# Experts ranked by their tokens, with a two-product path for the three smallest, in a two-layer transformer kernel

## The chip, the cores and the metric

The kernel runs on one core of one Trainium2 chip. The metric is the device time of one execution in microseconds (us). Three runs of the kernel before gave 1542.59, 1545.02 and 5386.56 us; their median is 1545.02 us. One further execution was profiled: it took 1542.61 us, and its span from the first to the last instruction is 1540.7 us.

## The reference

The program is a network of two layers on 256 tokens of 1024 channels, all in float32. Each layer is a mixer (two kinds of attention, a convolution, gates, an output product) followed by a feed-forward part. In layer 0 that part is one dense SwiGLU of width 2816; in layer 1 it is a mixture of eight experts of the same width, of which each token takes the two with the highest router logits. The change is in layer 1's feed-forward part:

```
h = rms_norm(x, ffn_norm_g)                       # 256 tokens x 1024
logits = h @ w_router + b_router                  # 256 x 8
top_logits, top_idx = top_k(logits, 2); gates = softmax(top_logits)
for each expert e, on the tokens that chose it:
    y = (silu(xe @ w_gate[e]) * (xe @ w_up[e])) @ w_down[e]
    x[token] += gate[token, e] * y
```

There are 512 choices for eight experts. With the reference's own inputs the experts 0 to 7 are chosen by 55, 77, 81, 111, 36, 59, 35 and 58 tokens.

The weights of one expert are 3 x 1024 x 2816 float32 numbers, 34.6 MB; the eight have 276.8 MB, and each is read once from the chip's memory.

## The kernel before, in words

**Splitting.** Matrix products are made in a float32 mode of TensorE that keeps only part of the mantissa, so each operand is split into a high and a low part, and a product is the sum of three matmuls: high by high, low by high, high by low (`mm3`, lines 379 to 381). The tokens stand still in the array (a 128x128 tile) and 512 columns of weights stream past. The weights' split is made on the core, in pieces: ScalarE (ACT) copies a piece of the raw tile to its high part (line 248) and VectorE (DVE) subtracts to get the low part (line 252). In the profile these are `hi<-raw` and `lo<-raw`.

**The stream of weights.** `_Stream` holds one list of chunks in the order in which they are used. A chunk is 2048 columns on 128 partitions (1 MB), loaded by one DMA from SP's queue into a ring of raw tiles: 5, and 7 more once the dense part is over, in the expert stage 12. A chunk is split in two pieces of `UNIT` = 1024 columns. There are four buffers for high parts and four for low ones (`PART_BUFS`), and `AHEAD` = 3 pieces are split ahead of the one in use. `next` hands out a piece and at once issues the split of the piece three further on. A raw tile comes free when its second low part is made, and only then can SP issue the DMA that refills it.

**The experts.** `route` and its helpers (`turned`, `logits`, `choose`, `place`) make the router's choice at the end of layer 1's mixer and give each token a place among the tokens of its expert (`slots`, `sels`). `moe` then goes through the experts 0 to 7 in order. Each is computed with 128 places, however many tokens it has; a conditional second pass at the end handles an expert with more than 128. For two experts at a time `gather` (line 991) builds one-hot matrices `pm` by comparing places with a row of numbers, and multiplies the split tokens `xhi`, `xlo` by them on TensorE (`xgp`, line 1009). Its result is scaled by the norm's gain and split again (lines 444 and 445, `xg`). `backward` transposes `pm` for the way back.

For each expert, gate and up products come in five blocks of 512 columns and one of 256 of each. A block's gate product `eg` takes 8 steps of 128 channels, 24 matmuls, then 24 for the up product `eu`. ACT makes the silu (line 1074), DVE multiplies gate by up (line 1079), four transposes `eaT` on TensorE (line 1065) turn the result, and ACT and DVE split it (`ehl`). The product with `w_down` then takes 22 steps of two halves, 132 matmuls `ed`. An expert has 396 matmuls of 512 columns and 66 pieces of weights to split. Its result is split (`yhi`, `ylo`) and scattered to the tokens' rows by 8 matmuls `sc`; ACT scales and GpSimd (POOL) adds to `x` (lines 1045, 1046), but for the last expert, where DVE does both.

**Order.** `tick` is called after each piece; `later(n, f)` puts `f` behind the n-th tick from then. So small work, such as transposes, is laid between the matmuls. Instructions of an engine run in the order in which the scheduler put them; TensorE, ACT, DVE, POOL and SP each have their own.

Of the kernel before, what the change touches and what calls it, by code (L numbers as in the profile page):

```python
# [36 lines left out]
MORE_BUFS = 7  # L37
AHEAD = 3
WARM = 7
MOE_SLABS = 8  # L40
SHARE = ((0,0),(1,0),(0,1),(1,1))
OUT_LAST = 3
CONV_RATE = 8 / 3
EARLY = (1, 1)
FIRST_LO = (-1, -1)
# [18 lines left out]
C_DIST = C_IOTA + S  # L64
# [16 lines left out]
def _constants():  # L81
# [14 lines left out]
    c[:, C_IOTA:C_IOTA + S] = k  # L96
    return c
# [17 lines left out]
def _chunks():  # L115
# [13 lines left out]
    def swiglu(key, names, i, by_half):  # L129
# [5 lines left out]
        if by_half:  # L135
            for h in range(2):
                k0s = list(range(0, FT, 4)) if h == 0 else [*range(0, FT - 6, 4), *range(FT - 6, FT, 2)]
                for k0, k1 in zip(k0s, k0s[1:] + [FT]):
                    out.append((key + "_dh", [(wd, i, k0, k1 - k0, h * 512, 512)], k1 - k0, 512))
        else:  # L140
            rows(key + "_d", wd, i, FT)

    for l in range(L):
# [16 lines left out]
        if l == 0:  # L160
            swiglu("f", ("w_ffn_gate", "w_ffn_up", "w_ffn_down"), 0, False)
    first_expert = len(out)
    for e in range(NE):
        swiglu("e", ("w_exp_gate", "w_exp_up", "w_exp_down"), (0, e), e == NE - 1)
    return out, first_expert


def _stream(h):
# [3 lines left out]
    chunks, _ = _chunks()  # L172
    flat = np.empty(sum(P * kn * n for _, _, kn, n in chunks), np.float32)
    at = 0
    for _, parts, kn, n in chunks:
        view = flat[at:at + P * kn * n].reshape(P, kn, n)
        at += P * kn * n
        c = 0
        for name, i, k0, k, c0, w in parts:
            a = h[name][i][k0 * P:(k0 + k) * P, c0:c0 + w]  # L180
            view[:, :, c:c + w] = a.reshape(k, P, w).transpose(1, 0, 2)
            c += w
# [16 lines left out]
class _Stream:  # L199
# [3 lines left out]
    UNIT = UNIT  # L203

    def __init__(self, tc, raw_pool, part_pool, ahead):
# [8 lines left out]
        self.more_pool = None  # L214
        self.hold = None
        self.lo_late = None
        self.turn = -1
        self.made = 0
        self.used = 0
# [8 lines left out]
    def add(self, key, src, kn, n):  # L228

        ci = len(self.plan)  # L230
        self.plan.append((src, kn, n))
        ku = self.UNIT // n
# [3 lines left out]
    def _make(self):  # L236
        nc = self.nc
        key, ci, u, ku, n = self.units[self.made]
        self.made += 1
        src, kn, _ = self.plan[ci]  # L240
        if ci not in self.raws:
            raw = self.raw_tile([P, kn * n])
            nc.sync.dma_start(raw, src)
            self.raws = {ci: raw}
        part = self.raws[ci][:, u * self.UNIT:(u + 1) * self.UNIT]
        hi = self.part_pool.tile([P, self.UNIT], F32R, tag="hi", name="hi")
        lo = self.part_pool.tile([P, self.UNIT], F32R, tag="lo", name="lo")
# [7 lines left out]
        return (key, hi.rearrange("p (k n) -> p k n", n=n), lo.rearrange("p (k n) -> p k n", n=n))  # L255
# [18 lines left out]
    def _fill(self):  # L274
        while (self.made < len(self.units) and self.made - self.used < self.ahead
               and self.units[self.made][0] != self.hold):
            self.queue.append(self._make())

    def next(self, key):
        if not self.queue:  # L280
            self.queue.append(self._make())
        k, hi, lo = self.queue.pop(0)
        assert k == key, (k, key)
        self.used += 1
# [5 lines left out]
def tile_kernel(ctx, tc, x, weights, columns, consts, out, dbg=None):  # L290
# [54 lines left out]
    onesr = cst.tile([P, P], F32R, name="onesr")  # L345
    half = cst.tile([P, 16], F32, name="half")
# [19 lines left out]
    chunks, first_expert = _chunks()  # L366
    places = [0]
    for _, _, kn, n in chunks:
        places.append(places[-1] + P * kn * n)

    def plan_chunks(start):
        for (key, _, kn, n), at in zip(chunks[start:], places[start:]):
            ws.add(key, weights[at:at + P * kn * n].rearrange("(p x) -> p x", p=P), kn, n)

    plan_chunks(0)
# [507 lines left out]
    def route(t, h):  # L883

        if (t, h) == (0, 0):
            rt.update(wrg=moe_weights(), hi=hp.tile([P, TT, D], F32R, tag="hhi", name="xhi"),
                      lo=hp.tile([P, TT, D], F32R, tag="hlo", name="xlo"), xT=[], rs=[], rs2=[], lg=[], late=[], sels=[], picks=[],
                      slots=[])
        if (t, h) == (1, 0):
            turned(0)  # L890
        if (t, h) == (1, 1):
# [4 lines left out]
            rt["late"][1](dve_)  # L896
            place(0)
            choose(1)
            place(1)

    def turned(t):
# [3 lines left out]
        late = rt["late"]  # L905
        if t == 1:
            late.extend(ws.begin(EARLY[0]))
        for q in range(2):
# [4 lines left out]
            (act_.copy if q else dve_.tensor_copy)(tl[:, 4 * q:4 * q + 4, :].rearrange("p k s -> p (k s)"), b)  # L913
        dve_.tensor_scalar(rs, rs, 1.0 / D, EPS, op0=ALU.mult, op1=ALU.add)
        pool_.tensor_tensor(rs, rs, half[:, :1], op=ALU.pow)
        if t == 1:
            late.extend(ws.begin(EARLY[1]))
            late[0](pool_)
# [3 lines left out]
        hi, lo = rt["hi"][:, t, :], rt["lo"][:, t, :]  # L922
        act_.activation(hi, xs[t], AF.Copy)
        pool_.tensor_tensor(lo, xs[t], hi.bitcast(F32), op=ALU.subtract)
        if t == 1:
            late.extend(ws.begin(PART_BUFS - len(late)))
# [42 lines left out]
    def moe():  # L969
        hhi, hlo, rs2, sels, picks, slots = (rt[k] for k in ("hi", "lo", "rs2", "sels", "picks", "slots"))  # L970


# [21 lines left out]
        def gather(e0, s0, late=()):  # L994

            pm = work.tile([P, TT, 2, P], F32R, tag="pm", name="pm", bufs=1)
            for t in range(TT):
                for i in range(2):
                    dve.tensor_scalar(pm[:, t, i, :], con[:, C_IOTA + s0:C_IOTA + s0 + P],
# [199 lines left out]
```

## Time and profile before

| what | value |
|---|---|
| median of three runs | 1545.02 us |
| profiled execution, device time | 1542.61 us |
| its span | 1540.7 us |
| TensorE, matmuls (PE) busy | 1495.4 us, 97% |
| DVE busy | 1236.7 us, 80% |
| ACT busy | 1024.2 us, 66% |
| bytes moved by DMA | 399.73 MB |
| first matmul of the first expert | 749.84 us |
| last `yhi` of the last expert | 1531.47 us |

A duration of a matmul in the profile includes the time in which it overlaps with the next, so the spacing of the starts, not the busy time, tells how fast TensorE goes. "Idle before" is the time that an engine stood still ahead of an instruction, and the name behind the arrow is what ended it.

### The profile page before, as it was taken

To read this page: it belongs to the slowest core of one execution; us is meant where nothing else is said; L and a number is where in the kernel's file an instruction comes from. 1 tells how busy PE (TensorE), PEld (TensorE's weight loads), DVE (VectorE), ACT (ScalarE), POOL (GpSimd) and SP (SyncE) were. 2 spreads that over 40 slices of the span, in tenths; PEclk is the share of its full clock that TensorE was granted. 3 is DMA by queue.
4 is the path that set the end of the run, shared out by engine and by line. 5 is a ranking of instruction groups with operands and counts; after the bars stand their busy time and mean duration, and the time that the engine had idled before them with its cause. 6 is when DMAs were issued, how large, how long until landed. Compare 5 with 4: busy or idle time off the path is not lost.

```text
span 1540.7 us, 19299 instructions
## 1 busy us (share of the span) xinstructions
PE 1495.4 (97%) x7080; PEld 1223.5 (79%) x7080; DVE 1236.7 (80%) x1519; ACT 1024.2 (66%) x1275; POOL 93.0 (6%) x70
## 2 busy tenths in 40 slices
PE   9989999999999989999899999999999999999997
PEld 7867788788887777788788888888878878778786
DVE  5898657655546798666898989989899989899897
ACT  6646653544335557653787888877777777777775
POOL 0200000000000200000100202001010010100100
PEclk9999999999999999999899999999999999999999
DMA  8343345455455343448599989998989989899881
GB/s 353 137 164 137 137 159 190 171 191 184 175 195 183 137 164 111 159 168 316 205 381 369 347 320 363 380 372 338 342 325 369 371 338 352 332 348 379 342 328 44
DMA packets 56551, 399.73 MB, mean 259 GB/s; under 512 B 6400, under 2 KB 6656, under 8 KB 8704
## 3 DMA queue, kind: packets, MB, share of 16 engines
q1 hardware_dynamic: 56160, 398.32, 68.7%
q8 instruction: 57, 0.93, 0.2%
q14 instruction: 46, 0.38, 0.1%
q10 hardware_dynamic: 288, 0.10, 0.0%
HBM read 397.34 MB, written 1.05 MB: 259 GB/s over the span
## 4 chain that ended last, share of the span: by engine, by line
PE 84%; DVE 8%; ACT 4%; POOL 2%; issue 1%; DMA 0%; SPq 0%; DVEq 0%; ACTq 0%
PE ed L379 5%; PE ed L380 5%; PE ed L381 5%; PE eg L381 5%; PE eg L379 5%; PE eg L380 5%; PE eu L381 5%; PE eu L379 4%; PE eu L380 4%; DVE lo L252 3%; PE gt L379 2%; PE gt L381 2%; PE gt L380 2%; DVE acc L539 2%; ACT hi L248 2%
## 5 line engine op out<-in xcount | busy, mean ns | idle before, releaser
L252 DVE TENSOR_TENSOR lo<-raw,hi 128x1024 fp32r<-128x1024 f32 x750 | 906.9, 1245 | 226.3 <-ACT hi L248 207.5
L248 ACT ACTIVATE hi<-raw 128x1024 fp32r<-128x1024 f32 x754 | 770.0, 1057 | 309.2 <-PE ed L380 36.0
L379 PE MATMUL eg<-hi,xg 128*128 128x512 f32 x384 | 153.8, 401 | 0.0
L381 PE MATMUL eg<-lo,xg 128*128 128x512 f32 x384 | 150.4, 392 | 0.0
L380 PE MATMUL eg<-hi,xg 128*128 128x512 f32 x384 | 149.7, 390 | 0.0
L379 PE MATMUL ed<-hi,ehl 128*128 128x512 f32 x352 | 138.2, 393 | 0.0
L380 PE MATMUL ed<-hi,ehl 128*128 128x512 f32 x352 | 137.8, 392 | 0.0
L381 PE MATMUL ed<-lo,ehl 128*128 128x512 f32 x352 | 133.6, 391 | 0.0
L381 PE MATMUL eu<-lo,xg 128*128 128x512 f32 x320 | 126.8, 396 | 6.5 <-DVE lo L252 6.5
L379 PE MATMUL eu<-hi,xg 128*128 128x512 f32 x320 | 125.4, 392 | 0.0
L380 PE MATMUL eu<-hi,xg 128*128 128x512 f32 x320 | 125.0, 391 | 0.0
L539 DVE SCALAR_TENSOR_TENSOR acc<-uT,cols,acc 128x255 f32<-128x255 f32 (+29 forms) x240 | 97.2, 465 | 0.0
L1046 POOL TENSOR_TENSOR x<-x,add 128x512 f32<-128x512 f32 x28 | 54.0, 1958 | 650.1 <-ACT add L1045 650.1
L381 PEld LDWEIGHTS eg<-lo,xg 128*128 128x128 f32 x384 | 72.1, 188 | 15.9 <-DVE lo L252 0.2
L380 PEld LDWEIGHTS eg<-hi,xg 128*128 128x128 f32 x384 | 72.4, 189 | 14.0 <-DVE xg L445 0.2
L379 PEld LDWEIGHTS eg<-hi,xg 128*128 128x128 f32 x384 | 72.2, 188 | 13.4
L381 PEld LDWEIGHTS eu<-lo,xg 128*128 128x128 f32 x320 | 60.1, 188 | 26.1 <-DVE lo L252 12.8
L381 PEld LDWEIGHTS ed<-lo,ehl 128*128 128x128 f32 x352 | 66.1, 188 | 13.7
L379 PE MATMUL gt<-hi,hhi 128*128 128x512 f32 x192 | 76.8, 400 | 0.0
L380 PEld LDWEIGHTS ed<-hi,ehl 128*128 128x128 f32 x352 | 66.2, 188 | 13.2
L379 PEld LDWEIGHTS ed<-hi,ehl 128*128 128x128 f32 x352 | 66.2, 188 | 13.0
L381 PE MATMUL gt<-lo,hhi 128*128 128x512 f32 x192 | 75.6, 394 | 0.0
(273 smaller groups left out, 2489.2 us busy)
## 6 DMA issues: line engine op xcount, KB each, us to landing
raw<-in_weights_dram SPq DMA_DIRECT2D x373, 1024.0 KB, 5.5
raw<-in_weights_dram SPq DMA_DIRECT2D x8, 512.0 KB, 5.3
x<-in_x_dram SPq DMA_DIRECT2D x2, 512.0 KB, 4.3
out_dram<-x SPq DMA_DIRECT2D x4, 256.0 KB, 2.5
att<-in_consts_dram SPq DMA_DIRECT2D x1, 448.0 KB, 6.9
con<-in_consts_dram SPq DMA_DIRECT2D x1, 256.0 KB, 6.2
cols<-in_columns_dram SPq DMA_DIRECT2D x1, 160.0 KB, 7.1
con<-in_consts_dram ACTq DMA_DIRECT2D x1, 64.0 KB, 4.0
```

Of the source, the lines that this page charges most:

```text
L248: ins = nc.scalar.activation(hi, part, AF.Copy)
L252: nc.vector.tensor_tensor(lo, part, hi.bitcast(F32), op=ALU.subtract)
L379: pe.matmul(dst, ahi, whi, start=first, stop=False)
L380: pe.matmul(dst, alo, whi, start=False, stop=False)
L381: pe.matmul(dst, ahi, wlo, start=False, stop=last)
L539: dve.scalar_tensor_tensor(acc[:, c, lag:], uT[:, c, :S - lag], w, acc[:, c, lag:], op0=ALU.mult, op1=ALU.add)
L1046: pool.tensor_tensor(xs[t][:, sl], xs[t][:, sl], add, op=ALU.add)
```

## The change

- **Ranks.** After the routing, `count` ranks the experts on the core: the experts 0 and 1 always get ranks 0 and 1, and the other six follow by falling number of tokens. DVE makes the order (`ranked`) and moves places and gates into it. The experts are computed in the order of ranks 0, 1, 5, 2, 6, 3, 4, 7.
- **Addresses from a register.** From the third expert on, which expert is loaded is known only on the core. SP reads its number from `ranked` into a register (`expert_of`), and the DMAs of that expert take their address from it. The weights of the experts are laid out in an array of their own, one row per expert.
- **64 places, two products.** The experts of ranks 5, 6 and 7 have 64 places. The high and the low part of their tokens stand side by side in the 128 columns of the still operand, so two matmuls, by the high and by the low part of the weights, give all four products. The lower half of the result is then copied by ACT (`low`) and added to the upper half by one matmul with a shifted identity (`fold`). In the down product no fold is needed: the scatter matrix has each place twice. If one of these three has more than 64 tokens, or another expert more than 128, a second pass goes over all eight experts.
- **Pieces of 2048 columns.** The experts' weights are split in pieces of 2048 columns, one per chunk, but for the first four and for the ends of the down product. Six buffers of that size hold three pairs of high and low parts; two pieces are split ahead. The raw ring has 11 tiles instead of 12.
- **The gather takes scaled tokens.** The gain is multiplied into the tokens before they are split (`xgain`, by DVE in `route`, with a table `gain` that one DMA loads). The gather's high and low matmuls go to separate columns of a bank, and one ACT copy of 512 or 384 columns takes both: DVE no longer splits `xg`. But for the first, a gather is spread over four ticks. The subtractions `xlo` move from POOL to DVE, as does the one low part of weights that POOL made there.

Cut to its core (`...` stands for lines left out):

```diff
-MORE_BUFS = 7
-AHEAD = 3
+MORE_BUFS = 6
+MORE_PARTS = 2
+AHEAD = 3 * 1024
+AHEAD_E = 2 * 2048
...
+UNIT_E = 2048
+SHORT = P // 2
+
+RANKS = (0, 1, 5, 2, 6, 3, 4, 7)
+SHORTS = (5, 6, 7)
...
+    def part_tile(self, name):
+
+        n = PART_BUFS + (MORE_PARTS if self.more_parts else 0)
+        self.part_turn = (self.part_turn + 1) % n
+        pool = self.part_pool if self.part_turn < PART_BUFS else self.more_parts
+        return pool.tile([P, UNIT_E], F32R, tag="part", name=name)
...
-            nc.sync.dma_start(raw, src)
+            nc.sync.dma_start(raw, src() if callable(src) else src)
...
+    def expert_of(rank):
+
+        if rank not in order["reg"]:
+            order["reg"][rank] = nc.values_load(order["idx"][0:1, rank:rank + 1], engines=(mybir.EngineType.SP,),
+                                                min_val=0, max_val=NE - 1)
+        return order["reg"][rank]
...
+                    flat = experts[bass.ds(expert_of(rank), 1), at:end].rearrange("o (p x) -> (o p) x", p=P)
...
+        if h == 0:
+            rt["xg"].append(T([P, D], "xgain"))
+        sl = slice(h * 512, (h + 1) * 512)
+        dve_.tensor_tensor(rt["xg"][t][:, sl], xs[t][:, sl], rt["gain"][:, sl], op=ALU.mult)
...
+    def low(t):
+        dve_.tensor_tensor(rt["lo"][:, t, :], rt["xg"][t], rt["hi"][:, t, :].bitcast(F32), op=ALU.subtract)
...
-            late[0](pool_)
...
-        pool_.tensor_tensor(lo, xs[t], hi.bitcast(F32), op=ALU.subtract)
...
-                    split_evac(hi, lo, b[:, j * S:(j + 1) * S], col(R_FG + KT + k))
...
+                    act.activation(xg[kp][:, j, :], b[:, :2 * width], AF.Copy)
...
+            def products(b, whi, wlo, lhs, first, last):
+                if short:
+                    pe.matmul(b, lhs(0), whi, start=first, stop=False)
+                    pe.matmul(b, lhs(0), wlo, start=False, stop=last)
+                else:
+                    mm3(b, lhs(0), lhs(1), whi, wlo, first, last)
...
+                        if k == KT and short:
+                            low = work.tile([P, 512], F32R, tag="low", name="low", bufs=2)
+                            act.activation(low[SHORT:], b[SHORT:], AF.Copy)
+
+                            def folded():
+                                pe.matmul(b, fold[SHORT:], low[SHORT:], start=False, stop=True, skip_group_check=True)
+                                then()
+                            later(2, folded)
...
+            dve.scalar_tensor_tensor(key, b[:, :NE], 8.0, con[:, C_KEY:C_KEY + NE], op0=ALU.mult, op1=ALU.add)
+            dve.max(top, key)
+            dve.max_index(idx, top, key)
...
-        with tc.If(most > P):
-            plan_chunks(first_expert)
-            all_experts(P, gather(0, P))
...
+        with tc.If(most > 0):
+            order["reg"] = {}
+            plan_experts()
+            all_experts(gather([(0, False), (1, False)], order["rest"], True), [0, 1], lambda: order["rest"], ())
```

How the instructions move, at three places. The first is ACT within the gate and up products of one block. Before, in expert 1 (`hi` is a piece of 1024 columns, `ea` the silu, `ehl` the turned block):

```order
L441 ACTIVATE ehl<-eaT 128x512
L248 ACTIVATE hi<-raw 128x1024 x2
L1074 ACTIVATE ea<-eg,rss 128x512
L248 ACTIVATE hi<-raw 128x1024 x6
L441 ACTIVATE ehl<-eaT 128x512
```

And now, in the first expert with 64 places, the third that is computed (`low` is the lower half of a product on its way to the fold):

```order
L1180 ACTIVATE low<-eg 64x512
L509 ACTIVATE ehl<-eaT 128x4x64
L284 ACTIVATE hi<-raw 128x2048
L1210 ACTIVATE ea<-eg,rss 64x512
L284 ACTIVATE hi<-raw 128x2048
L1180 ACTIVATE low<-eu 64x512
L284 ACTIVATE hi<-raw 128x2048 x3
```

Between two blocks stood eight pieces of 1024 columns, and now four or five of 2048; two instructions `low` stand among them.

The second place is DVE at the routing, behind the last residual sum. Before (`fi` and `sel` belong to the choice of the two experts, `slot` to the places, `pm` to the gather):

```order
L195 TENSOR_TENSOR x_89<-x_89,wo 128x512
L195 COPY xTf<-xTr 128x512
L195 CAST fi<-idx 128x2
L195 SCALAR_TENSOR_TENSOR sel_6015<-con,fi,s_6014 128x8
L195 TENSOR_TENSOR lo<-raw,hi 128x1024
L999 TENSOR_SCALAR pm<-con,slot_6036 128x128 x2
L195 TENSOR_TENSOR lo<-raw,hi 128x1024 x2
L445 SCALAR_TENSOR_TENSOR xg_6053<-xgp,cols,xg_6051 128x256 x2
```

And now:

```order
L219 TENSOR_TENSOR xlo<-xgain,xhi 128x1024
L219 TENSOR_TENSOR x_89<-x_89,wo 128x512
L219 TENSOR_TENSOR xgain<-x_89,gain 128x512
L219 COPY xTf<-xTr 128x512
L219 CAST fi<-idx 128x2
L1079 TENSOR_SCALAR pm<-con,slot_5817 128x128 x2
L219 TENSOR_TENSOR xlo<-xgain,xhi 128x1024
L219 TENSOR_TENSOR hilo<-raw,hilo 128x1024 x4
```

Two subtractions `xlo` and the products `xgain` came to DVE; the low part of weights between `sel` and the places went behind `pm`, and the splits of `xg` are gone.

The third place is SP's queue at the start of the third expert, where before the DMAs simply followed one another (`raw<-in_weights_dram` without anything between). Now:

```order
L276 DMA raw<-in_experts_dram 128x1024 x2
L412 TENSOR_LOAD ranked
L412 ISA x2
L276 ISA
L276 DMA raw<-in_experts_dram 128x2048
```

The expert's number is read once per expert, and one further instruction, `ISA`, stands ahead of each DMA.

## Rows read from the trace of the kernel before

**Rows 1.** The page's DMA issues: tiles, queue, count, KB each, us to landing.

```profile
raw<-in_weights_dram SPq DMA_DIRECT2D x373, 1024.0 KB, 5.5
```

**Rows 2.** Stages: from:to us, length, busy us by engine, granted clock, DMA share, GB/s.

```profile
8.00:12.00 4.00, 2.76 (x12) 1.79 (x11) 3.41 (x5) 4.00 (x8) 0.94 (x1) 1.00 1.04 400
...
720.00:730.00 10.00, 10.00 (x50) 8.39 (x49) 4.58 (x6) 2.61 (x4) 0.00 (x0) 1.00 1.01 423
740.00:750.00 10.00, 6.86 (x36) 6.75 (x37) 7.72 (x22) 2.75 (x8) 0.67 (x1) 0.59 0.46 162
800.00:900.00 100.00, 99.63 (x450) 81.94 (x449) 92.94 (x85) 81.45 (x90) 8.48 (x4) 1.00 0.96 359
```

**Rows 3.** Timeline of ACT: the first `yhi` of experts 0 to 4 and 6, start us first.

```profile
842.47 0.60 ACT L441 ACTIVATE yhi<-ed 128x512 fp32r<-128x512 f32 x1 [0.26 <-PE ed L381]
...
942.15 0.60 ACT L441 ACTIVATE yhi<-ed 128x512 fp32r<-128x512 f32 x1 [0.26 <-PE ed L381]
...
1037.13 0.60 ACT L441 ACTIVATE yhi<-ed 128x512 fp32r<-128x512 f32 x1 [0.26 <-PE ed L381]
...
1138.44 1.09 ACT L441 ACTIVATE yhi<-ed 128x512 fp32r<-128x512 f32 x2 [1.39 <-PE ed L381]
...
1235.26 1.09 ACT L441 ACTIVATE yhi<-ed 128x512 fp32r<-128x512 f32 x2 [1.88 <-PE ed L381]
...
1433.54 1.09 ACT L441 ACTIVATE yhi<-ed 128x512 fp32r<-128x512 f32 x2 [1.88 <-PE ed L381]
```

**Rows 4.** Timeline of PE in expert 1's up and gate products.

```profile
900.10 0.39 PE L381 MATMUL eu<-lo,xg 128*128 128x512 f32 x1
...
902.82 0.39 PE L381 MATMUL eg<-lo,xg 128*128 128x512 f32 x1
...
905.09 0.60 PE L1065 MATMUL eaT<-con,ea 128*128 128x128 f32 x4
...
905.45 0.47 PE L379 MATMUL eg<-hi,xg 128*128 128x512 f32 x1
```

**Rows 5.** Groups of DVE, 900 to 1400 us: count, busy us, mean ns, idle before.

```profile
L252 DVE TENSOR_TENSOR lo<-raw,hi 128x1024 fp32r<-128x1024 f32 x333 | 403.7, 1259 | 33.6 <-ACT hi L248 31.4
L1079 DVE SCALAR_TENSOR_TENSOR ea<-eu,rss,ea 128x512 f32<-128x512 f32 x26 | 19.3, 744 | 0.3 <-PE eu L381 0.3
L442 DVE TENSOR_TENSOR ehl<-eaT,ehl 128x512 fp32r<-128x512 f32 x25 | 17.2, 689 | 2.8 <-ACT ehl L441 1.2
...
L442 DVE TENSOR_TENSOR ehl<-eaT,ehl 128x256 fp32r<-128x256 f32 x5 | 2.1, 418 | 0.0
```

**Rows 6.** Timeline of DVE: four low parts back to back.

```profile
1184.03 4.63 DVE L252 TENSOR_TENSOR lo<-raw,hi 128x1024 fp32r<-128x1024 f32 x4 [0.50 <-ACT hi L248]
```

**Rows 7.** Groups of ACT, 900 to 1400 us, columns as in rows 5.

```profile
L248 ACT ACTIVATE hi<-raw 128x1024 fp32r<-128x1024 f32 x334 | 335.8, 1055 | 44.8 <-PE ed L380 24.4 <-PE eg L380 9.7 <-PE eu L380 7.2
L1074 ACT ACTIVATE ea<-eg,rss 128x512 f32<-128x512 f32 x25 | 17.1, 684 | 4.5 <-PE eg L381 4.5
L441 ACT ACTIVATE ehl<-eaT 128x512 fp32r<-128x512 f32 x25 | 14.9, 595 | 41.1 <-PE eaT L1065 39.7 <-PE ed L381 1.4
```

**Rows 8.** Timeline of all engines at the routing, and the first expert matmul.

```profile
735.61 2.36 POOL L195 TENSOR_TENSOR lo<-raw,hi 128x1024 fp32r<-128x1024 f32 x1
735.66 2.33 DVE L195 CAST fi<-idx 128x2 f32<-128x2 uint32 x1
...
738.30 2.39 DVE L195 SCALAR_TENSOR_TENSOR sel<-con,fi,s 128x8 fp32r<-128x8 f32 x1
738.33 2.34 POOL L195 TENSOR_TENSOR xlo<-x,xhi 128x1024 fp32r<-128x1024 f32 x1
...
742.95 0.17 DVE L195 CAST fi<-idx 128x2 f32<-128x2 uint32 x1
...
749.84 0.40 PE L379 MATMUL eg<-hi,xg 128*128 128x512 f32 x1
```

**Rows 9.** Waits of SP's queue, 760 to 1500 us: total us, times, longest.

```profile
SPq L243 <- DVE lo L252: 630.2, 245, 7.7
```

More of the change, by code (lines that the diff above doesn't have):

```diff
@@ L134, in swiglu @@
         proj(key + "_gu", [(wg, i, DFF - 256), (wu, i, DFF - 256)], 256)
[L135 to L141, printed above, removed]
+        rows(key + "_d", wd, i, FT)
     for l in range(L):
@@ L274, in _fill @@
     def _fill(self):
[L275 to L276 removed]
+        while (self.made < len(self.units) and self.units[self.made][0] != self.hold
+               and self.waiting + self.units[self.made][3] * self.units[self.made][4] <= self.ahead):
             self.queue.append(self._make())
@@ L289, in tile_kernel @@
 @with_exitstack
-def tile_kernel(ctx, tc, x, weights, columns, consts, out, dbg=None):
+def tile_kernel(ctx, tc, x, weights, experts, columns, consts, gains, out, dbg=None):
     nc = tc.nc
@@ new lines, in gather, with part @@
+            pts, rss = [], []
+            for fn in late:
+                fn(dve_)
+            for kp in range(KT // 2):
+                if at_once:
+                    piece(kp)
+                else:
+                    later(1 + kp, lambda kp=kp: piece(kp))
+            later(1 if at_once else 1 + KT // 2, lambda: backward(pm, pts, rss))
+            def part(i, q, k):
+                row = xg[k // 2][:, k % 2, :]
+                if pair[i][1]:
+                    return row[:, P:2 * P]
+                at = q * width + i * P if not short else q * (2 * width - P)
+                return row[:, at:at + P]
@@ L1035, in backward, with scatter @@
                 rss.append(r1)
-        def scatter(e, pt, yhi, ylo, h):
+        def scatter(gate, last, pt, yhi, ylo, h):
             sl = slice(h * 512, (h + 1) * 512)
@@ L1111, in moe, with all_experts, of @@
         gs = []
-        def all_experts(s0, got):
-            for e in range(NE):
-                xg, pts, rss = got
-                more = e % 2 and e + 1 < NE
-                nxt = expert(e, xg, pts, rss, lambda: gather(e + 1, s0) if more else None)
-                got = nxt or got
-        first = gather(0, 0, rt["late"][2:])
-        later(2, lambda: gs.extend(weigh()))
-        top = small.tile([P, 1], F32, tag="cnt", name="cnt", bufs=1)
-        cnt = small.tile([P, 1], I32, tag="cnti", name="cnti", bufs=1)
+        def all_experts(got, pair, slots, shorts):
+            ranks = RANKS
+            for p in range(NE):
+                r = ranks[p]
+                part, pts, rss = got
+                gate = (lambda t, r=r: order["gs"][t][:, r:r + 1]) if p >= 2 else (lambda t, r=r: gs[t][:, r:r + 1])
+                nxt = expert(pair.index(r), r in shorts, part, pts, rss, gate, p == NE - 1,
+                             (lambda q=of(p + 1, shorts): (gather([(c, c in shorts) for c in q], slots()), q))
+                             if p % 2 and p + 1 < NE else lambda: None)
+                if nxt:
+                    got, pair = nxt
+        def of(p, shorts):
+            return sorted(RANKS[p:p + 2], key=lambda r: r in shorts)
+        first = gather([(0, False), (1, False)], slots, True, [low_1, *rt["late"]])
+        later(1, lambda: gs.extend(weigh()))
+        over = cst.tile([P, 1], F32, name="over")
+        overi = cst.tile([P, 1], I32, name="overi")
         def count():
@@ new lines, in count @@
+            for t in range(TT):
+                order["slots"].append(ranked(f"slotr{t}", slots[t]))
+                order["gs"].append(ranked(f"gr{t}", gs[t]))
+            cap = con[:, C_CAP:C_CAP + NE]
+            for t in range(TT):
+                rest = cst.tile([P, NE], F32, name=f"rest{t}")
+                dve.tensor_tensor(rest, order["slots"][t], cap, op=ALU.subtract)
+                order["rest"].append(rest)
+            n = small.tile([P, NE], F32, tag="nr", name="nr", bufs=1)
```

320 lines of the change are left out of this document (209 added, 111 removed).

## The prediction

> **What bounds the kernel now.** I read the stages first. In the 100 us from 800 on, in the middle of the experts, TensorE has work nearly all the time, DVE is busy 92.9 us of 100, ACT 81.5, and the DMA engines run at 359 GB/s [rows 2]. So the change must be priced in the expert stage, and there on three engines at once. SP is the one that waits: 630 us in total, 245 times, for DVE to free a raw tile [rows 9]. The loads are therefore held back by the splits, not the other way round.
>
> The pace of TensorE comes from its starts. From 900.10 to 902.82 there are 12 matmuls of 512 columns, so one takes 2.72/12 = 0.227 us; four transposes take 905.45 - 905.09 = 0.36 us [rows 4]. An expert has 396 matmuls (89.8 us), 22 transposes (2.0) and 8 scatter matmuls (1.8): 93.6 us. The starts of `yhi` give what an expert really takes [rows 3]: 95.0 us (to 1037.13), 96.8 (to 1235.26), and 99.7 and 101.3 for those at whose end the gather for the next pair is made; the two from 1235.26 to 1433.54 take 198.3 together. Without a gather an expert takes about 96.2 us, 2.6 more than its TensorE work; with one about 101. So **TensorE bounds the experts**, and DVE is just behind it: 66 low parts at 403.7/333 = 1.212 us [rows 5] are 80.0 us, and `ea`, `ehl` and `ylo` bring it to about 89.
>
> **Short experts.** They are computed third, fifth and last: places where no gather stands in the expert of before, so the base is 96.2 us each.
>
> TensorE: 264 matmuls instead of 396 and 11 folds, 275 x 0.227 = 62.4, transposes at most 2.0, scatter 1.8: 66 us. It loses its place as the bound, since the weights to split are the same.
>
> DVE: no row shows a low part of 2048 columns. Back to back, four of 1024 take 4.63 us, 1.157 each [rows 6]. Going from 512 columns (`ehl`, 0.689) to 1024 (1.157 to 1.212) adds some 0.5; that is at least 0.468 and at most 1.212 - 0.53 = 0.68 for each 512. By the lower slope 2048 columns take 1.157 + 2 x 0.468 = 2.09 us, by no saving at all 2 x 1.212 = 2.42. I take 2.22: the four in a row leave out the 0.06 or so by which neighbours overlap, and 1024 columns at DVE's slope of (1.219 - 0.689)/512, 1.219 being one of the many undisturbed ones among the 333, add 1.06. Then 32 x 2.22 + 2 x 1.157 = 73.4; five `ea` (0.744) and five `ehl` of 256 columns (0.418), 5.8; the last block 0.8, `ylo` 1.4. POOL's sums run beside DVE as before and cost it (1.212 - 1.157) x 66 = 3.6 per expert. Together 85.0 us, between 81 and 91 by the two ends.
>
> ACT: a high part of 1024 takes 335.8/334 = 1.005 us; 512 columns less would be about 0.595 [rows 7], so 2048 take 1.005 + 2 x 0.457 = 1.92, and 2.01 at most. That is 63.4 with the two small ones, 11 `low` at the price of a 512-column `ehl` (0.595) 6.5, silu 3.9, `ehl` 2.2, `yhi` and the scaled rows 4.0: 80 us, 83 at most. ACT is not the bound, but close.
>
> Does the ring of three pairs let DVE run through? A high part three pieces on waits for TensorE to finish a piece. From the end of a low part: 1.82 us of matmuls, 1.92 of ACT and two hand-overs of some 0.1, 3.9 us; meanwhile DVE has two more pieces, 4.4. A spare of 0.5 us per round. In ACT's order `low`, and in some rounds `ehl`, stands ahead of that high part: 0.6 to 1.0 us late, but DVE has then `ea` or `ehl` of its own (0.4 to 0.7) to do in the gap. I allow 1 us per expert: **86 us**, a gain of 10.2 each, 30.6 for three.
>
> **Full experts.** TensorE still has 93.6 us. DVE falls from about 89 to 73.4 + 7.2 + 0.9 + 1.4 + 3.6 = 86.5, and loses the eight splits of `xg`. The ring is tighter: 2.72 + 1.92 + 2.22 against 3 x 2.72, a spare of 1.1 us after two hand-overs of 0.1, where four pieces of half the size had 4 x 1.36 - 1.36 - 1.00 - 1.16 - 0.2 = 1.7. In a block of 11.25 us DVE has 10.2 to do instead of 8 x 1.157 + 1.3 = 10.6. I take 1 us off each for the lighter DVE and the spread gather (192 columns where a short expert is in the pair): 5 us for five; the ends are 0 and 2 each.
>
> **Routing.** The two small instructions `fi` and `sel` took 2.33 and 2.39 us exactly while POOL worked on 1024 columns; the same `fi` without POOL took 0.17 [rows 8]. The change takes these three operations from POOL: 2 x 2.16 = 4.3 us off the chain to the first expert matmul at 749.84. Added on it: one `xlo` of 1.2 us ahead of the gather, and about 0.3 because the first `xlo` stands ahead of the last residual sum. The `xgain` products (0.69 each) fall into DVE's idle time between residual sums, if the `gain` table (0.5 MB behind three raw tiles, some 9 us at the 423 GB/s of this stretch [rows 2]) has landed. So 2.8 us gained. The ranking adds some 30 DVE instructions of about 0.2 us (0.17 to 0.23 for the small ones in rows 8): 6 us in the first three blocks, where DVE has about 1 us per block to spare: 3 us lost. The two cancel.
>
> **Loads.** The bytes stay the same. A short expert asks 34.6 MB/86 us = 402 GB/s; the chip gave 400 to 423 GB/s in two stretches [rows 2]. The whole stage asks about 370, and eight or nine tiles of the ring (1 MB each) bridge the short experts, though the ring has one less. The address from a register is bounded below by nothing, since a landing of 5.5 us [rows 1] is hidden by those tiles; above, if each of six experts drained the ring once for a landing, by 33 us. I take nothing: the number is ready in the first expert and wanted at the end of the second. The Trainium skill ("DMA: Bandwidth & Descriptors", section "Specifications") gives about 358 GB/s as what one core gets from HBM. An estimate from that page: in 86 us 30.8 MB come, each short expert lacks 3.8 MB, three use up what the ring holds, and the sum would be some 5 to 10 us higher. The stretches at 400 to 423 GB/s [rows 2] speak against that limit here.
>
> **Sum.** The profiled execution took 1542.61: - 30.6 - 5 + 0 = **1507 us**. The median of the runs, 1545.02, lies 2.4 above it, so I give 1508. By the good ends (83 us per short expert, 2 per full) it is 1493.
>
> A measurement of this kernel tells 2%, 31 us, from no change: faster means below 1514.
>
> **Rivals.**
>
> *The ring of three pairs binds* (0.24). If a round's parts cannot overlap, four pieces of a short block take 4/3 x (1.82 + 1.92 + 2.22 + three hand-overs of 0.26, as ACT waits ahead of `yhi` [rows 3]) plus ACT's extras of 2.2: 11.1 instead of 9.9 us. Over 5.5 blocks, 7 us each, 93 us per short expert, and the full ones gain nothing: 1542.6 - 3 x 3.2 + 5 = **1538**. For it: `low` waits for TensorE at the head of ACT's queue. Against: in most rounds two high parts are already queued ahead of it.
>
> *The clock falls in the short experts* (0.07). TensorE will stand still about 0.5 us of every 2.3. If the granted clock then drops from 2.4 to 1.2 GHz, a matmul takes 0.45 us, 275 of them 125 us, with the rest 129: 43 more than my 86, three times, **1635**. It decides from the point where TensorE needs more than DVE, that is above 0.31 us per matmul. For it: the clock was at 0.59 where TensorE was busy 6.9 of 10 us in the routing [rows 2]. Against: it was at 1.00 with TensorE busy 2.76 of 4 us at the start [rows 2], and at the routing the gap was of several us, not of half a one. The Trainium skill ("TensorE: Matmul & The Clock Gate", section "A second HAM failure mode: psum-queue depth-cycling") says that micro-idles between groups of matmuls make the clock go up and down between its two levels. By that rule this rival would be the likely case; the row at the start does not bear it out.
>
> *Late loads* (0.08). Reading the address costs a landing per expert, or the engines give no more than the 359 GB/s of the stretch from 800 on: 1515 to **1540**.
>
> *The change does not do what it says* (0.02). With the reference's inputs the ranks 5, 6 and 7 have 58, 36 and 35 tokens and the fullest expert 111, so there is no second pass. With other inputs there could be one, and it would cost another 750 us, some **2260**.
>
> The forecast case, 1490 to 1520, has 0.59; about 0.05 of it lies above 1514.
>
> Faster 0.54, same 0.37, slower 0.09. The range is 1490 to 1540: it takes in the ring and the late loads, and leaves out the clock, the second pass and the tails.
>
> **What would show it.** Right: `lo<-raw` of 2048 columns at 2.2 to 2.3 us; `yhi` of the short experts 84 to 88 us after the one before, with DVE over 95% busy, TensorE about 77% and the clock at 1.00; full experts at 94 to 100; `fi` and `sel` at 0.2 us. The ring would show as idle time of DVE before `lo<-raw` ended by ACT, above 5 us in a short expert; late loads as high parts waiting for DMA; the clock as matmul starts 0.45 us apart.

## The result, and the profile after

The changed kernel takes **1557.22 us** (median of four runs, 1555.62 to 1559.35), the kernel before 1543.8 in runs beside it: a ratio of 1.009, 95% interval 1.007 to 1.011. It is slower by 0.9%, less than the 2% that count as a change, and 49 us above the forecast of 1508, outside its range.

The profiled execution has a span of 1557.6 us, 16.9 more than before. First, when the last output product `wo` of the dense part started: one row of before, one of after (`hilo` is one tile that holds both parts of a small piece); the numbers behind the colon are the least, median and greatest duration in ns, then come the first and the last start.

```profile
L379 PE MATMUL wo<-hi,m x64: 388/390/501, 251.7 to 731.2; 128*128 128x512 f32 x64
```

```profile
L447 PE MATMUL wo<-hilo,m x64: 388/394/502, 254.8 to 737.1; 128*128 128x512 f32 x64
```

The routing behind it, in the timeline of after; these rows answer to [rows 8].

```profile
741.58 0.17 DVE L219 CAST fi<-idx 128x2 f32<-128x2 uint32 x1
...
742.05 0.23 DVE L219 SCALAR_TENSOR_TENSOR sel<-con,fi,s 128x8 fp32r<-128x8 f32 x1
...
747.05 1.22 DVE L219 TENSOR_TENSOR xlo<-xgain,xhi 128x1024 fp32r<-128x1024 f32 x1
...
751.31 0.56 PE L447 MATMUL eg<-hilo,xg 128*128 128x512 f32 x1
```

And the second `yhi` of each expert in the order of computing, which answers to [rows 3] (there the first one stands; the second follows 2.4 us later or is in the same row).

```profile
849.57 0.59 ACT L509 ACTIVATE yhi<-ed 128x512 fp32r<-128x512 f32 x1
...
950.14 0.59 ACT L509 ACTIVATE yhi<-ed 128x512 fp32r<-128x512 f32 x1
...
1042.20 0.60 ACT L509 ACTIVATE yhi<-ed 128x512 fp32r<-128x512 f32 x1
...
1144.19 0.58 ACT L509 ACTIVATE yhi<-ed 128x512 fp32r<-128x512 f32 x1
...
1246.51 0.60 ACT L509 ACTIVATE yhi<-ed 128x512 fp32r<-128x512 f32 x1
...
1348.43 0.58 ACT L509 ACTIVATE yhi<-ed 128x512 fp32r<-128x512 f32 x1
...
1443.48 0.60 ACT L509 ACTIVATE yhi<-ed 128x512 fp32r<-128x512 f32 x1 [0.80 <-PE ed L449]
...
1548.67 0.60 ACT L509 ACTIVATE yhi<-ed 128x512 fp32r<-128x512 f32 x1 [4.14 <-PE ed L1165]
```

The balance: the dense part ends 5.9 us later; from there to the first expert matmul it is 14.2 us instead of 18.6, -4.4; from that matmul to the last `yhi` 797.4 instead of 781.6, +15.7; the tail -0.3. Together 16.9. In the experts the three short ones, which were to take 86 us, took 92.1 (to 1042.20), 102.3 (to 1246.51) and 105.2 (to 1548.67). A `yhi` stands in ACT's queue and can itself be held up there: from the last matmul `ed` of one expert to that of the next it is 88.8, 99.1 and 105.2.

Two things in the profile were not foreseen. **The matmuls stand further apart.** In after, in a product of a full expert (compare [rows 4]):

```profile
1371.67 0.39 PE L447 MATMUL eg<-hi,xg 128*128 128x512 f32 x1
...
1374.47 0.27 PE L1194 MATMUL eaT<-con,ea 128*128 128x128 f32 x1
```

Twelve matmuls take 2.80 us, 0.2333 each; before they took 2.72. It is so in the feed-forward's down product `fd` too, and in `br` and `wo`, whose matmuls did not change, but not in the projections (`gt`, `ug`, `qk`), whose still operand lies in another pool.

**DVE waits for ACT, which waits for TensorE.** Waits of DVE in the third short expert, 1443 to 1548 us (total us, times, longest), and then those of ACT:

```profile
DVE lo L288 <- ACT hi L284: 18.6, 19, 2.1
```

```profile
ACT low L1180 <- PE eg L1165: 10.6, 5, 2.2
ACT low L1180 <- PE eu L1165: 8.2, 5, 1.8
```

In the first short expert DVE's wait is 8.8 us, in the second 15.2. The timeline of ACT in the third shows what happens:

```profile
1466.93 1.90 ACT L284 ACTIVATE hi<-raw 128x2048 fp32r<-128x2048 f32 x1
1470.64 0.59 ACT L1180 ACTIVATE low<-eu 64x512 fp32r<-64x512 f32 x1 [1.81 <-PE eu L1165]
1471.26 3.72 ACT L284 ACTIVATE hi<-raw 128x2048 fp32r<-128x2048 f32 x2
1475.00 0.38 ACT L509 ACTIVATE ehl<-eaT 128x256 fp32r<-128x256 f32 x1
1477.47 0.59 ACT L1180 ACTIVATE low<-eg 64x512 fp32r<-64x512 f32 x1 [2.09 <-PE eg L1165]
1478.09 1.91 ACT L284 ACTIVATE hi<-raw 128x2048 fp32r<-128x2048 f32 x1
```

ACT stands 1.81 and 2.09 us at `low`, which waits for the last matmul of a product; the `hi` behind it then starts without any wait. That `hi` is then missing: DVE stands for the one of 1478.09 with no other low part to make, and TensorE stops in turn when it has used up the one piece that was ready.

```profile
1480.04 2.29 DVE L288 TENSOR_TENSOR lo<-raw,hi 128x2048 fp32r<-128x2048 f32 x1 [2.00 <-ACT hi L284]
...
1482.38 0.50 PE L1165 MATMUL eu<-lo,xg 128*128 128x512 f32 x1 [1.72 <-DVE lo L288]
```

The Trainium skill ("PSUM — Partial Sum Buffer", section "Engine vs sequencer instructions") says that ACT's queue is strictly first in, first out; the rows of ACT agree.

The sizes of the splits were forecast well; these groups of after (900 to 1400 us) answer to [rows 5, 7]:

```profile
L288 DVE TENSOR_TENSOR lo<-raw,hi 128x2048 fp32r<-128x2048 f32 x161 | 371.9, 2327 | 65.8 <-ACT hi L284 60.0 <-PE eu L448 3.0 <-DMA raw<-in_experts_dram 2.3
L284 ACT ACTIVATE hi<-raw 128x2048 fp32r<-128x2048 f32 x161 | 306.5, 1914 | 48.4 <-PE ed L448 19.5 <-PE eg L448 12.0 <-PE eu L448 11.1
```

Stages of after, the three short experts and then a full one, columns as in [rows 2]:

```profile
950.14:1042.20 92.06, 80.62 (x308) 53.98 (x307) 81.18 (x49) 76.59 (x65) 13.27 (x5) 0.98 0.94 367
1144.19:1246.51 102.32, 81.15 (x309) 55.44 (x308) 81.77 (x49) 76.32 (x66) 13.26 (x5) 0.97 0.87 336
1443.48:1548.67 105.19, 79.63 (x309) 52.84 (x307) 81.78 (x50) 75.50 (x64) 11.22 (x4) 1.00 0.64 238
1042.20:1144.19 101.99, 101.99 (x466) 83.00 (x466) 86.32 (x54) 76.53 (x62) 6.60 (x4) 0.99 0.92 348
```

In the short experts the granted clock is 0.97 to 1.00, that is the level of 2.4 GHz, and no engine is busy through: the 81 to 82 us of DVE's work are spread over 92, 102 and 105.

### The profile page after: what moved, and what is told of

It is laid out like the page before. It is cut to its first block, busy times and chain, and to the rows that moved or that the text cites. A ratio compares the mean times of both kernels' runs of the same rounds, so it can differ in the third digit from the quotient of the medians.

```text
span 1557.6 us, 18142 instructions
## 1 busy us (share of the span) xinstructions
PE 1466.9 (94%) x6717; PEld 1157.8 (74%) x6717; DVE 1194.0 (77%) x1261; ACT 1016.1 (65%) x1056; POOL 104.8 (7%) x69
## 4 chain that ended last, share of the span: by engine, by line
PE 69%; DVE 15%; ACT 6%; issue 4%; DMA 3%; POOL 2%; DVEq 0%; SPq 0%; ACTq 0%
DVE lo L288 5%; ACT hi L284 4%; DVE acc L607 4%; PE eg L449 4%; PE eg L447 4%; PE eg L448 4%; DVE hilo L288 3%; PE ed L447 3%; PE ed L448 3%; PE ed L449 3%; PE eu L447 3%; PE eu L449 3%; PE eu L448 3%; DMA raw<-in_experts_dram 3%; PE gt L449 2%
## 5 line engine op out<-in xcount | busy, mean ns | idle before, releaser
L288 DVE TENSOR_TENSOR lo<-raw,hi 128x2048 fp32r<-128x2048 f32 x253 | 583.7, 2321 | 102.7 <-ACT hi L284 95.7
L284 ACT ACTIVATE hi<-raw 128x2048 fp32r<-128x2048 f32 x253 | 481.8, 1914 | 84.4 <-PE ed L448 28.3
L288 DVE TENSOR_TENSOR hilo<-raw,hilo 128x1024 fp32r<-128x1024 f32 x244 | 295.3, 1222 | 178.3 <-ACT hilo L284 177.8
L284 ACT ACTIVATE hilo<-raw 128x1024 fp32r<-128x1024 f32 x248 | 258.1, 1059 | 239.1 <-PE fd L449 35.5
L1144 POOL TENSOR_TENSOR x<-x,add 128x512 f32<-128x512 f32 x28 | 72.4, 2614 | 644.9 <-ACT add L1143 644.9
L447 PE MATMUL eg<-hi,xg 128*128 128x512 f32 x232 | 94.7, 408 | 0.7 <-ACT hi L284 0.7
L448 PE MATMUL eg<-hi,xg 128*128 128x512 f32 x232 | 92.6, 399 | 0.0
L447 PE MATMUL ed<-hi,ehl 128*128 128x512 f32 x200 | 79.3, 397 | 0.0
L448 PE MATMUL ed<-hi,ehl 128*128 128x512 f32 x200 | 78.8, 394 | 0.0
L447 PE MATMUL eu<-hi,xg 128*128 128x512 f32 x200 | 78.7, 393 | 0.0
L448 PE MATMUL eu<-hi,xg 128*128 128x512 f32 x200 | 78.5, 393 | 0.0
L447 PE MATMUL gt<-hilo,hhi 128*128 128x512 f32 x192 | 76.9, 401 | 0.0
L449 PE MATMUL gt<-hilo,hhi 128*128 128x512 f32 x192 | 75.2, 392 | 0.0
L448 PE MATMUL gt<-hilo,hlo 128*128 128x512 f32 x192 | 75.0, 391 | 0.0
L1165 PE MATMUL eu<-lo,xg 128*128 128x512 f32 x120 | 51.5, 430 | 14.2 <-DVE lo L288 14.2
L1164 PE MATMUL eg<-hi,xg 128*128 128x512 f32 x144 | 57.5, 399 | 0.0
```

The source lines that it names most:

```text
L284: ins = nc.scalar.activation(hi, part, AF.Copy)
L288: nc.vector.tensor_tensor(lo, part, hi.bitcast(F32), op=ALU.subtract)
L447: pe.matmul(dst, ahi, whi, start=first, stop=False)
L448: pe.matmul(dst, alo, whi, start=False, stop=False)
L449: pe.matmul(dst, ahi, wlo, start=False, stop=last)
L1144: pool.tensor_tensor(xs[t][:, sl], xs[t][:, sl], add, op=ALU.add)
```

## The experiments

**Where the tiles lie.** In the program, the still operands of the experts' and row products lie in the pool `slab`, the split weights in `part` and `more_parts`. Modulo 256 bytes a partition, `slab` and the first four split tiles start at the same place in the kernel before; in the changed one `slab` stands 64 bytes off them, since the ranking's small tiles made the pool ahead of it 64 bytes longer. `hhi` and `hlo`, the projections' still operands, are 0 off in both. The edit in three kernels is one tile of 64, 192 or 448 bytes ahead of `slab`:

```diff
+    pad = small.tile([P, 16], F32, tag="pad", name="pad", bufs=1)
+    pool.memset(pad, 0.0)
     slab = ctx.enter_context(tc.tile_pool(name="slab", bufs=MOE_SLABS))
```

*aligned* (64 bytes, changed kernel).

> The changed kernel with one tile of 64 bytes a partition more, ahead of the pool whose tiles are the stationary operand of the experts' and the row products. In the changed kernel these tiles start at 32 modulo 128 bytes and four of the six split tiles at 96; in the kernel before all of them started at 96, and with the tile more they all do again. No instruction changes but one small memset. Theory A (the offset between the two operands sets the matmul spacing): the spacing of the experts' matmuls goes from 0.2333 us to 0.2267-0.228, that of br, w_out and the feed-forward's down product to 0.2267; the dense part gets 696 x 0.0066 = 4.6 us shorter, each of five full experts 396 x 2/3 x 0.0062 = 1.6; together -13 us, 1544 us. Theory B (the spacing comes from the longer splits or from other traffic): 0.2333 stays, 1557 us.

*before_shifted* (the same two lines in the kernel before).

> The kernel before with the same 64 bytes put ahead of the same pool, so that its stationary tiles move from 96 to 32 modulo 128 while every split tile stays at 96. Theory A: br, w_out, the feed-forward's down product and all experts' matmuls go from 0.2267 to 0.2333 us; the dense part +4.6 us, each of eight experts 396 x 0.0066 = +2.6; +25 us at most, 1560-1570 us. Theory B: nothing moves, 1544 us.

*aligned512* (`[P, 112]`).

> The changed kernel with a tile of 448 bytes a partition ahead of the pool of the stationary tiles, in place of the 64 of the run aligned: there the stationary tiles still stood 128 bytes off the first four split tiles modulo 512, and only the two later split tiles, equal modulo 512, had a unit of 12 matmuls at 0.2267-0.228 apart. Now all stand at 224 modulo 512. Theory A, mended (the offset must be zero modulo 256 or 512): experts' and row products' matmuls 0.2267-0.228 apart in every unit, the feed-forward's down product 0.2267; -4.6 us in the dense part, -1.6 per full expert, 1544 us. Theory B (it is not the offset): 0.2333 stays in two units of three, 1556 us.

*pad192* (`[P, 48]`).

> The changed kernel with a tile of 192 bytes ahead of the stationary tiles: they then stand 256 bytes off the first four split tiles modulo 512 (equal modulo 256) and equal modulo 512 to the last two. If equality modulo 256 is enough, all units of the experts are at 0.2267-0.228 and the down product of the feed-forward at 0.2267, 1544 us; if it must be 512, two units in three and the down product stay at 0.2333, 1556 us.

The text of the first was wrong on the modulus: 64 bytes more brought 128 bytes off, not zero. What was measured (`fd`: spacing of 12 matmuls of the feed-forward's down product):

| kernel | `slab` against splits 1 to 4, and 5 and 6, modulo 256 | `fd` spacing | time, ratio to before |
|---|---|---|---|
| before | 0 | 0.2267 us | 1542.65 |
| changed | 64, 0 | 0.2333 | 1557.22, 1.009 [1.007, 1.011] |
| aligned | 128, 0 | 0.2325 | 1556.25, 1.009 [1.007, 1.010] |
| pad192 | 0, 0 (256 modulo 512) | 0.2267 | 1545.14, one run |
| aligned512 | 0, 0 | 0.2267 | 1544.5, 1.001 [1.000, 1.002] |
| before_shifted | 64 | 0.2333 | 1561.3, 1.012 [1.010, 1.013] |

The timeline of before, and then of before_shifted, 12 matmuls apart:

```profile
430.74 0.39 PE L380 MATMUL fd<-hi,flo 128*128 128x512 f32 x1
...
433.46 0.39 PE L380 MATMUL fd<-hi,flo 128*128 128x512 f32 x1
```

```profile
430.68 0.40 PE L382 MATMUL fd<-hi,flo 128*128 128x512 f32 x1
...
433.48 0.40 PE L382 MATMUL fd<-hi,flo 128*128 128x512 f32 x1
```

2.72 against 2.80 us, with the same instructions. And the same for aligned512:

```profile
430.69 0.39 PE L449 MATMUL fd<-hilo,fhi 128*128 128x512 f32 x1
...
433.41 0.39 PE L449 MATMUL fd<-hilo,fhi 128*128 128x512 f32 x1
```

So the offset costs the changed kernel 12.7 us (1557.2 - 1544.5), by which it comes level with the kernel before, and puts 18.5 us on the kernel before (1561.3 - 1542.8 beside it; 25 at most were expected). In aligned512 the last of all matmuls `wo` starts at 732.97 instead of 737.58, the 4.6 us expected; most of the rest lies in the five full experts. That 64 and 128 bytes off both cost, and 0 does not, whether modulo 512 or 256, is shown; other offsets were not run, and why it costs is not shown. The Trainium skill ("SBUF — State Buffer", section "Who interferes with whom") names the port pair that DVE and GpSimd share as the only contention among the engines; these runs show one more dependence, on the addresses of TensorE's two operands.

**The order of ACT's queue.** In the built order, `low` of the first short expert has two or more pieces `hi` ahead of it that go beyond the piece it waits for in 10 of 11 cases, of the second in 4, of the third in 1; in the others just one. The place decides the wait: the 15 copies with two or more `hi` ahead wait 0.02 to 1.25 us, the 18 with one ahead 0.96 to 2.50, all but one of them 1.6 or more.

*low_behind* (on aligned). What is called by `act_` is pinned: it keeps the place in ACT's order that the program gives it. What is called by `act` is placed by the scheduler.

```diff
-                            act.activation(low[SHORT:], b[SHORT:], AF.Copy)
+                            act_.activation(low[SHORT:], b[SHORT:], AF.Copy)
```

> The aligned kernel, and the copy low of the short experts pinned on ACT's queue behind what was written ahead of it, which is hi of the second split after the one that low waits for. In the changed kernel 17 of 22 copies low of the second and third short expert stood with only one hi ahead of them; now all 33 stand behind two. Theory C (the queue's order costs the short experts their gain): DVE's idle time ended by ACT falls from 8-19 us to under 6 per short expert, the spacing of their ends from 92, 102 and 105 us to 87-91 each, 30-38 us less than the aligned kernel: 1507-1515 us. Rival D (three pairs of splits are too few whatever the order): the short experts stay at 98 or more, 1535-1545 us.

It took 1554.49 us, 1.008 [1.006, 1.010]; 1.8 less than aligned. The short experts took 91.6, 99.7 and 104.2. Theory C's gain did not come, and two of three short experts stayed above the 98 us of rival D. The waits of ACT in the second short expert (1142 to 1241) say why:

```profile
ACT ehl L511 <- PE eaT L1196: 8.5, 3, 2.8
ACT ea L1212 <- PE eg L1185: 4.5, 4, 2.7
...
ACT low L219 <- PE eg L1167: 0.6, 1, 0.6
```

`low` no longer waits, but `ehl` and `ea`, which also wait for TensorE, now stand at the head with a `hi` behind them.

*pins* (on aligned512: `low` as above, `ehl` of the short experts, and `ea` of all):

```diff
-                    act.activation(a[rows], bg[rows, :n], AF.Silu, scale=r1())
+                    act_.activation(a[rows], bg[rows, :n], AF.Silu, scale=r1())
...
-                    split_evac(hl[:, :, :SHORT], hl[:, :, SHORT:], src)
+                    split_evac(hl[:, :, :SHORT], hl[:, :, SHORT:], src, on=act_)
```

> The run aligned512 with low, ea and ehl of the experts all pinned on ACT's queue behind what was written ahead of them. In low_behind low no longer waited at the head of ACT's queue, but ehl did (16 us in the last short expert, behind it a hi whose tile was free), and DVE still lost 14-18 us per short expert to ACT. Theory C: with all three pinned no copy that waits for a matmul stands ahead of a hi that could run; DVE's idle ended by ACT falls under 6 us per short expert, their spacing to 88-92, 25-33 us less than aligned512. Rival D (three pairs of splits are too few whatever the order): short experts 95 or more, within 15 us of aligned512.

1515.79 us, 0.982 [0.981, 0.984]: 28.7 less than aligned512, inside what the order was expected to give. The second `yhi` around the first and the second short expert:

```profile
942.92 0.59 ACT L511 ACTIVATE yhi<-ed 128x512 fp32r<-128x512 f32 x1
...
1032.33 0.61 ACT L511 ACTIVATE yhi<-ed 128x512 fp32r<-128x512 f32 x1
...
1132.41 0.59 ACT L511 ACTIVATE yhi<-ed 128x512 fp32r<-128x512 f32 x1
...
1222.55 0.60 ACT L511 ACTIVATE yhi<-ed 128x512 fp32r<-128x512 f32 x1
```

89.4 and 90.1 us (91.1 and 101.0 in aligned512), and the third 89.7 (105.0). The five full experts take the same time in both (495.6 and 495.9): the gain is that of the short ones. DVE's idle time ended by ACT is 4.2, 4.5 and 5.9 us in the three, under the 6 expected. Rival D, which had 95 us or more per short expert with three pairs, is refuted.

*pins_only* (the pins without the tile).

> The changed kernel, with its own addresses and three pairs, and low, ea and ehl pinned. The pins brought 28.7 us on the aligned kernel. If the two losses are apart, 1557.2 - 28.7 = 1528.5, within 4 us. If the pins work only where the operands are aligned, 1540 or more.

1528.91 us, 0.990 [0.989, 0.992]: 28.3 under the changed kernel. The two losses add.

**The number of pairs.** *al_ring4* and *pins_ring4*:

```diff
-MORE_BUFS = 6
-MORE_PARTS = 2
+MORE_BUFS = 4
+MORE_PARTS = 4
...
-AHEAD_E = 2 * 2048
+AHEAD_E = 3 * 2048
```

> The run aligned512 with four pairs of split tiles and two landing tiles fewer, nothing pinned: in the order that ACT's queue gets, most copies low of all three short experts still stand with one hi ahead. Theory C: the short experts stay at 95 or more, within 10 us of aligned512. Rival D: they fall under 92, 20 us or more under aligned512.

> The run pins with four pairs of split tiles in place of three (two landing tiles fewer, three splits ahead). Theory C alone: no gain over pins, 2 us either way. Rival D: the fourth pair is what brings the short experts to 86-89, 10 us or more under pins. If landing tiles bind, hi waits for DMA and the full experts get longer.

A fourth pair without the pins made it slower: 1554.94, 1.008 [1.006, 1.010], 10.4 above aligned512, and in ACT's order 23 of 33 copies `low` still had one `hi` ahead. The edit also takes two raw tiles away, but no `hi` or `lo` waits for DMA in the experts of al_ring4, so that is not the cause. With the pins the same edit brought 4.1 us, more than theory C's 2 and less than rival D's 10: 1511.66, 0.980 [0.979, 0.982]. So the depth of the ring is not what held the short experts, and helps a little once the order is right.

**The rest of the queue.** *pins_all* (on pins_ring4, `ehl` of the full experts and all `yhi` pinned too).

> The run pins_ring4 with the full experts' ehl and all yhi pinned on ACT's queue too. In pins_ring4 DVE still lost 55 us of the expert stage to ACT, while the unpinned ehl waited 44 us for its transposes. Theory C: what is left stands in full experts, where TensorE is busy through, so this brings little, 1506-1512 us. Rival: the waits of ehl in the full experts still cost there, 1500 us or less.

1502.99 us, 0.974 [0.972, 0.976]: **the best version, 2.6% faster than before**, and the only one that is clear of the 2%. It lies between theory C (1506 at least) and the rival (1500 at most). The second `yhi` can no longer be the measure here, since all `yhi` have another place in ACT's order; the last matmul `ed` ahead of each short expert and its own last one tell the length:

```profile
940.41 0.39 PE L451 MATMUL ed<-hilo,ehl 128*128 128x512 f32 x1
...
1025.20 0.39 PE L1167 MATMUL ed<-hilo,ehl 128*128 128x512 f32 x1
...
1126.25 0.39 PE L451 MATMUL ed<-hilo,ehl 128*128 128x512 f32 x1
...
1209.44 0.39 PE L1167 MATMUL ed<-hilo,ehl 128*128 128x512 f32 x1
...
1405.01 0.39 PE L451 MATMUL ed<-hilo,ehl 128*128 128x512 f32 x1
...
1489.33 0.40 PE L1167 MATMUL ed<-hilo,ehl 128*128 128x512 f32 x1
```

84.8, 83.2 and 84.3 us. So measured, the profiled executions compare as follows (us; the first expert counts from its first matmul; of the kernel before stand the experts in the same places of the order, with a gather at the end of the same ones):

| kernel | first, second, third short expert | five full experts together |
|---|---|---|
| before | 95.0, 96.6, 97.7 (not short) | 491.9 |
| changed | 88.8, 99.1, 105.2 | 503.8 |
| aligned512 | 88.0, 97.9, 105.0 | 495.9 |
| pins | 86.2, 87.0, 89.7 | 495.6 |
| pins_ring4 | 85.1, 83.2, 88.0 | 496.8 |
| pins_all | 84.8, 83.2, 84.3 | 491.7 |

From pins_ring4 to pins_all some 5 us come in the full experts, as the rival had it, and 4 in the short ones, most of that in the last. In the second short expert DVE waits 5.4 us for ACT (15.2 in the changed kernel); its row of waits, and its stage, columns as in [rows 2]:

```profile
DVE lo L288 <- ACT hi L284: 5.4, 5, 1.5
```

```profile
1126.25:1209.44 83.19, 77.54 (x306) 52.21 (x305) 76.96 (x47) 74.98 (x63) 9.52 (x4) 1.00 0.95 376
```

No `hi` or `lo` waits for DMA there, and SP waits 56.8 us for DVE: at 376 GB/s the loads still do not bind.

**What the short path is worth.** *all_full* (on aligned), *best_all_full* (on pins_ring4) and *ordered_full* (on pins_all):

```diff
-SHORTS = (5, 6, 7)
+SHORTS = ()
```

> The aligned kernel with no short expert: all eight take 128 slots and three products; ranks, register addresses, long splits and the gather of scaled tokens stay. Theory C: a short expert as built (92, 102, 105 us, mean 100) saves nothing against a full one (98-99 when aligned), so the time is that of the aligned kernel within 6 us: 1538-1546 us. If the short path had brought its forecast 10 us an expert, this would be 30 us slower than the aligned kernel, 1574 us.

> The run pins_ring4 with no short expert. With the queue in order the short experts took 86-88 us there, against 92-95 for a full expert that gathers nothing beside it. Theory C: the short path is now worth 3 x 6 to 9 us, 1530-1540 us. If the pins and the fourth pair had been the whole gain and not the short path, 1512 us.

> The run pins_all with no short expert, so that both kernels have the same ordered queues and only the short path differs; in best_all_full ehl and yhi of the full experts were not pinned, and its full experts took 94.9 to 104.5 us. If the short path is worth the forecast's 10.2 us each, 1503 + 31 = 1534 us; if the 13.8 us each by which best_all_full stands above pins_ring4 hold, 1544; if the pins on full experts bring what they brought in pins_all for each of eight, 1540.

1564.47 us (1.014 [1.012, 1.016]), 1553.05 (1.006 [1.004, 1.008]) and 1536.32 (0.996 [0.994, 0.997]). Against the kernel with short experts these are +8.2 (6 at most were expected), +41.4 and +33.3. As built, the short path saved 2.7 us an expert; in the ordered queue it saves 11.1. The expectation of 1530 to 1540 for the second was too low, since its full experts, unpinned with four pairs, were themselves longer.

## Why the prediction was wrong

**The step that failed** is that of the ring in the short experts: "0.6 to 1.0 us late", "I allow 1 us per expert". It took for `low` and `ehl` only their duration. What they cost is their wait for TensorE at the head of the queue, 1.6 to 2.5 us nearly each time that `low` has just one `hi` ahead of it, with a `hi` behind that could have run. DVE's idle time ended by ACT was 8.8, 15.2 and 18.6 us in the three, instead of 1; pinning three kinds of ACT's instructions, and nothing else, gave 28.7 us back. The rival of the ring named that mechanism, and was put aside with "in most rounds two high parts are already queued ahead of it". That is true of the first short expert, whose order stands ahead of the prediction (10 of 11, and it took 92.1 us), and false of the other two (5 of 22, 102.3 and 105.2). One expert's order was taken for all three.

**The rival's own size** was too small too: it had 93 us per short expert and 1538 us, and priced hand-overs, not the wait. What it said would show it, DVE's idle time ended by ACT above 5 us, came. Its name, a ring too small, was wrong: a fourth pair without the order made it slower.

**The second failure** is a term that is not in the sum. "TensorE still has 93.6 us" in a full expert, and nothing for the dense part, took the spacing of 0.227 us [rows 4] as the chip's. It was a property of where the tiles lay. This term is +12.7 us. Without it and with the pins the kernel stands at 1515.8, with pins_all at 1503.0, on both sides of the forecast of 1508.

**A third term** was mis-sized: 5 us off the full experts. Without the offset (aligned512) the five took 4.0 us more than five such experts before, and in pins_all as long as those: no run shows the lighter DVE or the spread gather shorten them.

In the profiled execution of the changed kernel, then, the short experts stand 3.8 us above the same three before instead of 30.6 below, the full ones 11.9 above instead of 5 below, of which 8 go with the offset.

**Right** were: the price of 2048 columns (2.22 and 1.92 forecast, 2.33 and 1.91 in the groups), though for ACT the step of 0.457 per 512 columns does not follow from its two figures, whose difference is 0.41; the short expert at 86, as soon as the queue lets it be (83.2 to 84.8), and its gain of 10.2 (11.1); `fi` and `sel` at 0.2 us (0.17, 0.23), for 4.4 us of routing, more than the 2.8 forecast. That the 86 came out is in part luck: DVE's work was 77 to 82 us in these stages and not 85, and in pins_all it stood idle for about 6 us and not 1, so it was busy 92 to 93% and not over 95. TensorE's records are busy 93% there and not 77, but they overlap. That pins_all comes within 5 us of 1508 is luck too: its short experts gained 37.0 us and not 30.6, its full ones nothing and not 5.

The clock did not fall: 0.97 to 1.00 in short experts with waits of up to 1.8 us for `lo`, so the rule of the Trainium skill weighed there ("TensorE: Matmul & The Clock Gate", section "A second HAM failure mode: psum-queue depth-cycling") would have misled here. Loads were not late: `lo` waits 2.3 us for DMA in 500. No second pass ran.

**Open**: what the ranking costs by itself (in aligned512 the first expert takes 1.4 us more than before, where 3 were forecast, but that holds more than the ranking), why the operands' addresses set the spacing, and why the scheduler's order is worse in the second and third short expert than in the first.

## What to carry to other kernels

An instruction that waits costs what stands behind it in its queue: when a copy from PSUM is added to an engine that also feeds the pipeline, look at its place in the order in every repetition, not in one, and pin all copies of that kind, since pinning one hands the wait to the next. When a change adds even 64 bytes of small tiles, compare the spacing of matmuls that it did not touch; if it moved, look at the operands' start addresses. Measure a stage by the engine that does its work, not by an instruction whose place in a queue the experiment changes. A gain that is not there in the total may be there in full behind two losses, of which one has nothing to do with it.

## What the runs showed of the hardware that was not expected

- The spacing of float32 matmuls of 512 columns, with a weight load each, depends on the start of the still operand against the moving one in a partition: 0.2267 us at 0 bytes modulo 256, 0.2325 to 0.2333 at 64 or 128. The durations in the records differ by 1.0 to 1.5% (390 and 394 to 396 ns), the spacing of the starts by 2.6 to 2.9%, so the starts must be compared.
- TensorE kept a granted clock of 0.97 to 1.00 over three stretches of about 100 us in which its records are busy for only some 80.
